# A gated attention and convolution block: channel sums accumulated in DRAM, and queue bounds in the output projection

## The chip, the cores and the metric

The kernel runs as one launch on one core of a Trainium2 chip. The core has a matrix engine (TensorE, PE in the profile, with its weight load PEld beside it), VectorE (DVE), ScalarE (ACT), GpSimd (POOL), and SyncE (SP), from which most transfers are issued. Transfers between DRAM and the on-chip memory SBUF run on 16 DMA engines, whichever engine issued them; PSUM is the small memory that PE writes its sums to. The metric is the device time of one execution in microseconds (us), lower is better.

## The reference

One decoder layer over 1024 tokens of width 1024, in float32. What matters here:

```
h = RMSNorm(x);  q, k, v, u, g = split(h @ w_in)
a = differential attention(q, k, v), 8 heads, RMS norm per head
y_a = a @ w_proj_attn
c = causal depthwise conv, width 31 (u_a * sigmoid(u_b)) + conv_b
c = silu(LayerNorm over the 1024 channels (c))
y_b = c @ w_proj_conv
x = x + (sigmoid(g_a) * y_a + sigmoid(g_b) * y_b) @ w_out
x = x + (silu(gate) * up) @ w_down,   gate, up = split(RMSNorm(x) @ w_gate_up)
```

The LayerNorm needs, for each token, the mean over all 1024 channels of the convolution's result. The channels lie in eight tiles of 128 partitions by 1024 tokens, so the mean begins with a sum over the eight tiles.

## The kernel before

**Products.** Each matrix product is made of three passes of PE over operands split in a high and a low part (hi*hi, hi*lo, lo*hi): `split_hi` (L120, on ACT) rounds a tile to its high part, `split_lo` (L125, on DVE) subtracts it from the tile for the low part. Weights arrive by DMA in a raw tile (`wraw`), are split into `whi` and `wlo` (three buffers each) and used; a `Stream` holds the splits two items ahead of their use (`ws.next()`). The output projection and the feed-forward use a seven-product scheme in place of eight block products, so that they also need sums and differences of blocks (`wless`, L1742, on DVE).

**Order.** The program's order is not the order in the queues: a planner that keeps simulated times puts the instructions of each engine in order, by what is ready in its simulation and by the place in the program. `after(ins)` adds one bound: what is traced under it is queued behind `ins`, if it is on the same engine. `last_mm`, `last_lo` and `last_of(engine)` name the latest PE product, low split or instruction of an engine. A queue, once made, runs strictly in its order.

**Convolution.** `conv_taps` (L565 to L589) handles one tile of 128 channels: `first_tap` (L575, ACT) writes the accumulator `acc`, 30 `tap`s (L581, DVE) add to it, and after the last one the result is stored to the DRAM tile `c_d[c]` (L587, SP). Tiles 0 to 3 have `acc` in PSUM and are copied first to an SBUF tile `done` (L585, ACT); tiles 4 to 7 have `acc` in SBUF. `done` and these `acc` share one tag with one buffer, so a tile's first tap waits until the tile before has left it. The taps are background work, handed out between the steps of the input projection and of attention, each lot behind the latest DVE instruction. In attention POOL does little but two small memsets per pair of query blocks (L1299 and L1300: one 128x128 block of each of `ph` and `pl`, the turned probabilities, is zeroed), which wait until the product `weigh` of the pair before has read these tiles.

**LayerNorm.** `ln_chunks(sb)` (from L1521) does one half of the tokens: it loads the eight tiles' halves `cc` from `c_d` (L1533), sums them into `s1` on DVE (L1535, seven additions), splits the sum and lets PE turn it into the mean, spread over the partitions (L1541). Then per tile: difference to the mean (L1547, DVE), square (L1548, ACT), its sum (L1551, DVE), and with the root scale, bias, sigmoid and product (L1566 to L1569) and the split to `cT_hi` and `cT_lo`. These steps are laid between the products of the attention projection, which has its own gates: `gated` (L1606, L1607) loads a gate and takes its sigmoid on ACT, `ya_out` (L1614) multiplies on DVE and so frees the PSUM tile. The first gates are bound behind `mean_hi`, the latest ACT instruction after the first step, which is the high split of the first half's `s1`. The convolution's projection follows on PE and reads `cT`, half after half.

**Output projection.** The loop over `WSEVEN` (from L1757) makes seven products z = 0 to 6 of 4 x 4 x 3 matmuls (L1804) into PSUM banks "a", "b" and "c"; "a" and "c" share four tiles, and after each product DVE adds the sums to the residual rows `xa` (L1814), which come by DMA (L1748). `wless` calls make weight differences at z = 1 and z = 3. From z = 5 on, `norm2` (L1699 to L1711) normalizes finished rows for the feed-forward: scale on DVE (L1703), transposes on PE (L1706), `split_hi` on ACT, `split_lo` on DVE, copy back on ACT (L1711). In z = 6 the `ws.next()` calls already split the first weights of the feed-forward (its gate product is L168 to L170 after the loop).

Of the kernel before, what the change touches and what calls it, by code (L numbers as in the profile page):

```python
# [10 lines left out]
F32 = mybir.dt.float32  # L11
F32R = mybir.dt.float32r
AF = mybir.ActivationFunctionType
ALU = mybir.AluOpType
AX = mybir.AxisListType

P = 128
S = 1024
# [39 lines left out]
def kernel(  # L58
# [321 lines left out]
    a_d = [dr.tile([P, S], F32, name=f"a_d{h}") for h in range(H)]  # L380
    u_d = [dr.tile([P, S], F32, name=f"u_d{c}") for c in range(NKT)]
    c_d = [dr.tile([P, S], F32, name=f"c_d{c}") for c in range(NKT)]
    g_d = [dr.tile([P, S], F32, name=f"g_d{c}") for c in range(2 * NKT)]
    ya_d = [dr.tile([P, S], F32, name=f"ya_d{c}") for c in range(NKT)]
    x2_d = [dr.tile([P, D], F32, name=f"x2_d{i}") for i in range(NT)]
# [181 lines left out]
    def conv_taps(c):  # L567
        acc = []

        def first_tap():  # L570
            if c < CONV_PSUM:
                acc.append(pcv[0].tile([P, S], F32, tag="acc", name=f"acc{c}", bufs=1))
            else:
                acc.append(cv.tile([P, S], F32, tag="acc", name=f"acc{c}", bufs=1))
            act.activation(acc[0][:], us[c][:], AF.Identity, bias=pcol("conv_b", c), scale=cw[:, c, CW - 1 : CW])  # L575

        def tap(t):
            def go():
                n = CW - 1 - t
                a_ = acc[0][:, n:]  # L580
                dve.scalar_tensor_tensor(a_, us[c][:, : S - n], cw[:, c, t : t + 1], a_, op0=ALU.mult, op1=ALU.add)  # L581
                if t == 0:
                    if c < CONV_PSUM:
                        done = cv.tile([P, S], F32, tag="acc", name=f"done{c}", bufs=1)
                        act.copy(done[:], acc[0][:])  # L585
                        acc[0] = done
                    nc.sync.dma_start(c_d[c][:], acc[0][:])  # L587

            return go  # L589

        return [first_tap] + [tap(t) for t in range(CW - 2, -1, -1)]
# [930 lines left out]
    def ln_chunks(sb):  # L1522

        cs = slice(sb * 512, (sb + 1) * 512)
        cc = [f32(cT_lo[:, c, cs]) for c in range(NKT)]

        def half(tag):
            return lp.tile([P, 512], F32, tag=tag, name=nm("ln" + tag), bufs=2)

        s1 = half("s")  # L1530
        for c in range(NKT):
            with after(last_at):
                nc.sync.dma_start(cc[c], c_d[c][:, cs])  # L1533
            if c:
                dve.tensor_tensor(s1[:], cc[0] if c == 1 else s1[:], cc[c], op=ALU.add)  # L1535
        mean = pm("mean") if sb else pln.tile([P, 512], F32, tag="mean", name=nm("mean"), bufs=1)
        s1h, s1l = [lp.tile([P, 512], F32R, tag="sq", name=nm(t_), bufs=2) for t_ in ("lnmh", "lnml")]
        split_hi(s1h[:], s1[:])
        split_lo(s1l[:], s1[:], s1h[:])
        for s_ in (s1h, s1l):  # L1540
            pe.matmul(mean[:], part[:], s_[:], start=s_ is s1h, stop=s_ is s1l)  # L1541
        yield
        s2 = half("s")
        for c in range(NKT):
            q = half("sq") if c else s2
            d = half("csg" if sb == 0 and c % 2 else "d")
            dve.tensor_tensor(d[:], cc[c], mean[:], op=ALU.subtract)  # L1547
            act.activation(q[:], d[:], AF.Square)  # L1548
            nc.sync.dma_start(cc[c], d[:])
            if c:  # L1550
                dve.tensor_tensor(s2[:], s2[:], q[:], op=ALU.add)  # L1551
            if c == 3:
                yield
        yield
        var = pm()
        for e in range(4):
            pe.matmul(var[:, e : e + 1], s2[:, e * P : (e + 1) * P], f32(part[:, 0:1]), start=True, stop=True)
        r = rsq8(var[:, :4], 1.0, 4)
        rb_ = pln.tile([P, 512], F32, tag="rstd", name=nm("rstd"), bufs=1)
        rw = half("sq")  # L1560
        dve.tensor_copy(rw[:].rearrange("p (e q) -> p e q", q=P), r.unsqueeze(2).to_broadcast([P, 4, P]))
        for e in range(4):
            pe.transpose(rb_[:, e * P : (e + 1) * P], rw[:, e * P : (e + 1) * P], ident[:])
        for c in range(NKT):
            z, sg = half("z"), half("csg")
            dve.tensor_tensor(z[:], cc[c], rb_[:], op=ALU.mult)  # L1566
            act.activation(z[:], z[:], AF.Identity, bias=pcol("ln_b", c), scale=pcol("ln_w", c))
            act.activation(sg[:], z[:], AF.Sigmoid)
            dve.tensor_tensor(z[:], z[:], sg[:], op=ALU.mult)  # L1569
            split_hi(cT_hi[:, c, cs], z[:])  # L1570
            split_lo(cT_lo[:, c, cs], z[:], cT_hi[:, c, cs])
            if c % 2:
                yield
# [120 lines left out]
    def rows_of(l):  # L1694
        s_ = ssq[l][0]
        dve.tensor_tensor(s_[:], s_[:], ssq[l][1][:], op=ALU.add)
        return rsq8(s_[:], 1.0 / D, 4)

    def norm2(t_, r, tp_):  # L1699

        for g in range(2):
            h = xa[t_][:, TOK[g]]
            dve.scalar_tensor_tensor(h, h, r[:, t_ % 4 : t_ % 4 + 1], wb2[:, TOK[g]], op0=ALU.mult, op1=ALU.mult)  # L1703
            pt = tp_()
            for k in range(4):
                pe.transpose(pt[:, k * P : (k + 1) * P], h[:, k * P : (k + 1) * P], ident[:])  # L1706
            src4 = pt[:].rearrange("p (k s) -> p k s", s=P)
            h_ = h2_hi[:, 4 * g : 4 * g + 4, t_ * P : (t_ + 1) * P]
            split_hi(h_, src4)
            split_lo(h2_lo[:, 4 * g : 4 * g + 4, t_ * P : (t_ + 1) * P], src4, h_)  # L1710
            act.copy(h, pt[:])  # L1711
# [48 lines left out]
    for z, (z_, b_, s_, (l, c), full) in enumerate(WSEVEN):  # L1760
        if z == 0:
            with after(last_of(mybir.EngineType.SP)):
                wload("12", (1, 0))
                wload("S3", (0, 1))
                wload("S1", (0, 0))
                wload("S4", (1, 1))
                x_rows(0)
                sload("S2")
                sload("S4")
                x_rows(1)  # L1770
                sload("S3")
        if z == 1:
            wless("S1", "S3", "S1")
        if z == 3:
            for q in range(2):
                room["22", q] = wraw()[:]
            wless("22", "12", "S2")
            for q in range(2):
                early_weights("22", q, 2 * q)
            wless("S3", "S4", "S3")  # L1780
        if z == 4:
            for j in (2, 3):
                early_weights("S3", j, 2 * j)
        start = s_ not in o
        if start:
            o[s_] = [p_.tile([P, 512], F32, tag=tag, name=nm("wo")) for p_, tag in wo_banks[s_]]
        for j in range(4):
            if z_ in ("S2", "S4", "S3") or j % 2 == 0:
                hi, lo = ws.next()
            if z == 1 and j == 2:  # L1790
                wless("S2", "S4", "S1")
            if z == 5 and j == 2:
                h2_hi = big.tile([P, NKT, S], F32R, tag="xhi", name="h2_hi")
                h2_lo = big.tile([P, NKT, S], F32R, tag="xlo", name="h2_lo")
            for i in range(4):
                t_ = slice(i * P, (i + 1) * P)
                if z_ in ("S2", "S4", "S3"):
                    A, B = [m_[:, t_] for m_ in (hi, lo)], [m_[:, 512:] for m_ in (hi, lo)]
                else:
                    r_, k_ = {"11": (0, 0), "12": (0, 1), "22": (1, 1), "S1": (1, 0)}[z_]  # L1800
                    A = [m_[2 * j + k_][:, TOK[r_]][:, t_] for m_ in (mT_hi, mT_lo)]
                    B = [m_[:, 512 * (j % 2) : 512 * (j % 2 + 1)] for m_ in (hi, lo)]
                for y_, (u_, v_) in enumerate(((0, 0), (0, 1), (1, 0))):
                    last_mm[0] = pe.matmul(  # L1804
                        o[s_][i][:], A[u_], B[v_], start=start and j + y_ == 0, stop=j == 3 and y_ == 2,
                        skip_group_check=not start,
                    ).ins
            for t_ in NORMS.get((z, j), ()):
                with after(last_mm[0]), after(last_add if z == 6 else None):
                    norm2(t_, r2[0], tr_first)  # L1810
        for i in range(4):
            t_ = 4 * l + i
            h = xa[t_][:, TOK[c]]
            last_add = dve.tensor_tensor(h, o[s_][i][:], h, op=ALU.add).ins  # L1814
            if full:
                nc.sync.dma_start(x2_d[t_][:, TOK[c]], h)
                squares(t_, c)
        if z in (4, 6):
            r2[l] = rows_of(l)
# [267 lines left out]
```

## Time and profile before

| | |
|---|---|
| three runs, median (lowest, highest) | 1738.96 us (1737.48, 1740.53) |
| the profiled execution, whole | 1737.98 us |
| its span, first to last instruction | 1736.2 us |
| mean granted TensorE clock | 0.999 |
| busy PE, PEld, DVE, ACT, POOL | 1718.1, 1479.1, 1283.6, 864.9, 211.7 us |

All times inside the execution are counted from the span's start. A group row names line, engine, operation, tiles and count, then busy time and mean duration in ns; a row of the timeline names start and duration in us, engine, line, operation, tiles and count, and in brackets the idle time of the engine before it and what ended that. In a row of a table by stage each engine's busy us stand in the order PE, PEld, DVE, ACT, POOL, each with its count in brackets, then the granted TensorE clock (1.00 is full), the DMA engines' busy share and GB/s.

In order of time: input projection with the first convolution tiles to about 310 us, attention with the others to about 822, attention projection with LayerNorm to 913, convolution's projection to about 1018, output projection to 1092, feed-forward to the end.

### The profile page before, as it was taken

The page shows a single profiled execution, that of the slowest core. Times are in us where ns is not written, and L with a number is a line of the kernel's source. Part 1 is how long each engine was busy: PE and PEld are TensorE (multiplying, and loading weights), DVE is VectorE, ACT ScalarE, POOL GpSimd, SP SyncE. Part 2 cuts the span into 40 slices and gives each one's busy share as a digit, 9 for nine tenths or more (in the row PEclk, how much of TensorE's full clock was granted, in tenths as well). Part 3 has the DMA queues.
Part 4 walks back from the last instruction along what each step waited for, and adds up shares of the span by engine and source line. Part 5 has one row for each costly group of instructions (what it writes and reads, how often), then busy time and mean ns, then how long its engine had stood idle before and what let it go on. Part 6 is the DMA issues. An engine that isn't in the chain of part 4 may idle for free.

```text
span 1736.2 us, 25867 instructions
## 1 busy us (share of the span) xinstructions
PE 1718.1 (99%) x9245; PEld 1479.1 (85%) x9245; DVE 1283.6 (74%) x2142; ACT 864.9 (50%) x1958; POOL 211.7 (12%) x200
## 2 busy tenths in 40 slices
PE   9999999999999999999999999999999999999999
PEld 7997889998998998988787878888888888888887
DVE  7575889898988988977788678866676666565554
ACT  5333335767776776856356325633333333333332
POOL 4997851000000000000000000000000000000000
PEclk9999999999999999999999999999999999999999
DMA  6343454334344344354873583135445444597663
GB/s 203 118 128 120 161 178 139 90 104 139 105 110 144 88 110 140 92 146 140 302 236 122 177 304 127 49 108 177 152 159 173 154 152 151 179 363 276 219 216 130
DMA packets 256325, 276.92 MB, mean 159 GB/s; under 512 B 16258, under 2 KB 178114, under 8 KB 256196
## 3 DMA queue, kind: packets, MB, share of 16 engines
q1 hardware_dynamic: 253920, 268.50, 48.2%
q0 software_dynamic: 1984, 5.72, 1.1%
q8 instruction: 73, 1.20, 0.3%
q10 hardware_dynamic: 292, 1.05, 0.1%
q14 instruction: 56, 0.46, 0.1%
HBM read 177.65 MB, written 81.30 MB: 149 GB/s over the span
## 4 chain that ended last, share of the span: by engine, by line
PE 89%; DVE 4%; DMA 3%; ACT 3%; issue 1%; SPq 0%; ACTq 0%; DVEq 0%
PE acc L962 30%; PE acc L481 12%; PE pg L170 11%; PE pg L168 11%; PE pg L169 11%; PE wo L1804 3%; PE sc L1271 2%; PE sc L1270 2%; PE pT L1309 2%; DVE acc L581 1%; PE pW L169 1%; PE pW L168 1%; PE pW L170 1%; PE pg L1088 1%; DMA room<-soS 1%
## 5 line engine op out<-in xcount | busy, mean ns | idle before, releaser
L581 DVE SCALAR_TENSOR_TENSOR acc<-u,cw,acc 128x1023 f32<-128x1023 f32 (+14 forms) x240 | 303.5, 1265 | 15.3 <-ACT acc L575 12.8
L168 PE MATMUL pg<-whi,hT_hi 128*128 128x256 f32 x704 | 199.9, 285 | 0.5 <-DVE v L125 0.5
L170 PE MATMUL pg<-whi,hT_lo 128*128 128x256 f32 x704 | 199.8, 284 | 0.0
L169 PE MATMUL pg<-wlo,hT_hi 128*128 128x256 f32 x704 | 199.4, 284 | 0.0
L125 DVE TENSOR_TENSOR wlo<-draw,whi 128x1024 fp32r<-128x1024 f32 x75 | 91.8, 1224 | 85.2 <-ACT whi L120 79.1
L120 ACT CAST whi<-draw 128x1024 fp32r<-128x1024 f32 x75 | 79.1, 1055 | 129.5 <-PE acc L481 119.3
L168 PEld LDWEIGHTS pg<-whi,hT_hi 128*128 128x128 f32 x704 | 133.9, 191 | 2.2 <-DVE v L125 0.7
L169 PEld LDWEIGHTS pg<-wlo,hT_hi 128*128 128x128 f32 x704 | 134.2, 191 | 1.8
L170 PEld LDWEIGHTS pg<-whi,hT_lo 128*128 128x128 f32 x704 | 134.2, 191 | 1.7
L120 ACT CAST whi<-wraw 128x1024 fp32r<-128x1024 f32 x90 | 94.5, 1052 | 73.0 <-PE pg L169 35.9
L481 PE MATMUL acc<-wlo,whi 128*128 128x512 f32 x308 | 119.8, 389 | 0.0
L481 PE MATMUL acc<-whi,wlo 128*128 128x512 f32 x308 | 119.8, 389 | 0.0
L168 PE MATMUL pg<-hT_hi,whi 128*128 128x512 f32 x288 | 114.6, 398 | 0.1
L169 PE MATMUL pg<-hT_lo,whi 128*128 128x512 f32 x288 | 114.1, 396 | 0.0
L170 PE MATMUL pg<-hT_hi,wlo 128*128 128x512 f32 x288 | 113.7, 395 | 0.0
L1277 ACT ACTIVATE E<-E,mn 128x640 f32<-128x640 f32 (+7 forms) x128 | 99.7, 779 | 27.6 <-DVE mn L1272 27.0
L120 ACT CAST whi<-s 128x1024 fp32r<-128x1024 f32 x54 | 56.8, 1052 | 107.2 <-PE acc L962 103.3
L125 DVE TENSOR_TENSOR wlo<-wraw,whi 128x1024 fp32r<-128x1024 f32 x75 | 92.5, 1236 | 12.7 <-ACT whi L120 12.0
L1272 DVE CUSTOM_DVE_ANT_0 E<-sc,tb 128x512 f32<-128x512 f32 (+3 forms) x128 | 74.2, 585 | 27.5 <-PE pT L1309 13.1
L962 PE MATMUL acc<-h_hi,whi 128*128 128x512 f32 x240 | 93.4, 389 | 0.0
L962 PE MATMUL acc<-h_lo,whi 128*128 128x512 f32 x240 | 93.4, 389 | 0.0
L962 PE MATMUL acc<-h_hi,wlo 128*128 128x512 f32 x240 | 90.1, 389 | 0.0
(371 smaller groups left out, 4587.8 us busy)
## 6 DMA issues: line engine op xcount, KB each, us to landing
wraw<-in_w_gate_up_dram SPq DMA_DIRECT2D x44, 512.0 KB, 4.8
wraw<-in_w_in_dram SPq DMA_DIRECT2D x40, 512.0 KB, 4.6
qs<-qs SPq DMA_DIRECT2D x96, 128.0 KB, 2.3
wd<-in_w_down_dram SPq DMA_DIRECT2D x44, 256.0 KB, 3.2
tdT<-wd SPq DMA_DIRECT2D x88, 128.0 KB, 4.7
draw<-sdS SPq DMA_DIRECT2D x44, 256.0 KB, 3.9
draw<-tdT SPq DMA_DIRECT2D x44, 256.0 KB, 3.7
wraw<-in_w_in_dram SPq DMA_DIRECT2D x32, 256.0 KB, 3.3
```

The lines of the kernel that those rows point to most:

```text
L120: act.copy(dst, src)
L125: last_lo[0] = dve.tensor_tensor(dst, src, f32(hi), op=ALU.subtract).ins
L168: pe.matmul(o, lh, rh, start=start, stop=False)
L169: pe.matmul(o, lh, rl, start=False, stop=False)
L170: last_mm[0] = pe.matmul(o, ll, rh, start=False, stop=stop).ins
L481: m = pe.matmul(o[s_][i][:], l_[:, ts], r_[:, 512:], start=start and j + y_ == 0, stop=j == n - 1 and y_ == 2, skip_group_check=not start,)
L581: dve.scalar_tensor_tensor(a_, us[c][:, : S - n], cw[:, c, t : t + 1], a_, op0=ALU.mult, op1=ALU.add)
L962: last_mm[0] = pe.matmul(o[:], a_[x_][:, k, :], b_[y_][:, k, :], start=start and k + x_ + y_ == 0, stop=k == 3 and x_ == 1, skip_group_che ...
L1270: pe.matmul(o[:, :w], qh[:, qs], k, start=True, stop=False)
L1272: dve.tensor_tensor_reduce(e[:, ks], o[:, :w], tb[:, S - nk + c0 : S - nk + c0 + w], 1.0, mn[:, j : j + 1] if c0 else 3.0e38, ALU.add, ALU ...
L1277: act.activation(e[:, :nk], e[:, :nk], AF.Exp, bias=mn[:, j : j + 1], scale=-1.0, accum_out=l[:, j : j + 1])
L1804: last_mm[0] = pe.matmul(o[s_][i][:], A[u_], B[v_], start=start and j + y_ == 0, stop=j == 3 and y_ == 2, skip_group_check=not start,).ins
```

## The change

- A new DRAM tile `cs_d` holds the sum over the eight convolution tiles. When a tile has ended it is stored to `c_d[c]` as before, and besides that tile 0 is stored to `cs_d` (SP), and tiles 1 to 7 are added to it by an accumulating DMA issued from POOL.
- `ln_chunks` loads `s1` from `cs_d` with one DMA, ahead of the eight loads of `cc`; the seven additions on DVE are gone, in both halves.
- In the output projection the `wless` of "22" (z = 3) and of "S2" (z = 1) are queued behind the latest low split.
- In z = 6, the DVE part of the splits that `ws.next()` makes is queued behind the latest DVE instruction, each matmul behind the one before it, and from the first `norm2` on each matmul of the loop behind the latest transpose.

```diff
--- before.py
+++ after.py
@@ -380,6 +380,7 @@
     a_d = [dr.tile([P, S], F32, name=f"a_d{h}") for h in range(H)]
     u_d = [dr.tile([P, S], F32, name=f"u_d{c}") for c in range(NKT)]
     c_d = [dr.tile([P, S], F32, name=f"c_d{c}") for c in range(NKT)]
+    cs_d = dr.tile([P, S], F32, name="cs_d")
     g_d = [dr.tile([P, S], F32, name=f"g_d{c}") for c in range(2 * NKT)]
     ya_d = [dr.tile([P, S], F32, name=f"ya_d{c}") for c in range(NKT)]
     x2_d = [dr.tile([P, D], F32, name=f"x2_d{i}") for i in range(NT)]
@@ -585,6 +586,10 @@
                         act.copy(done[:], acc[0][:])
                         acc[0] = done
                     nc.sync.dma_start(c_d[c][:], acc[0][:])
+                    if c:
+                        pool.dma_start(cs_d[:], acc[0][:], accum_op=ALU.add)
+                    else:
+                        nc.sync.dma_start(cs_d[:], acc[0][:])
 
             return go
 
@@ -1528,11 +1533,10 @@
             return lp.tile([P, 512], F32, tag=tag, name=nm("ln" + tag), bufs=2)
 
         s1 = half("s")
-        for c in range(NKT):
-            with after(last_at):
+        with after(last_at):
+            nc.sync.dma_start(s1[:], cs_d[:, cs])
+            for c in range(NKT):
                 nc.sync.dma_start(cc[c], c_d[c][:, cs])
-            if c:
-                dve.tensor_tensor(s1[:], cc[0] if c == 1 else s1[:], cc[c], op=ALU.add)
         mean = pm("mean") if sb else pln.tile([P, 512], F32, tag="mean", name=nm("mean"), bufs=1)
         s1h, s1l = [lp.tile([P, 512], F32R, tag="sq", name=nm(t_), bufs=2) for t_ in ("lnmh", "lnml")]
         split_hi(s1h[:], s1[:])
@@ -1696,6 +1700,8 @@
         dve.tensor_tensor(s_[:], s_[:], ssq[l][1][:], op=ALU.add)
         return rsq8(s_[:], 1.0 / D, 4)
 
+    last_tr = [None]
+
     def norm2(t_, r, tp_):
 
         for g in range(2):
@@ -1703,7 +1709,7 @@
             dve.scalar_tensor_tensor(h, h, r[:, t_ % 4 : t_ % 4 + 1], wb2[:, TOK[g]], op0=ALU.mult, op1=ALU.mult)
             pt = tp_()
             for k in range(4):
-                pe.transpose(pt[:, k * P : (k + 1) * P], h[:, k * P : (k + 1) * P], ident[:])
+                last_tr[0] = pe.transpose(pt[:, k * P : (k + 1) * P], h[:, k * P : (k + 1) * P], ident[:]).ins
             src4 = pt[:].rearrange("p (k s) -> p k s", s=P)
             h_ = h2_hi[:, 4 * g : 4 * g + 4, t_ * P : (t_ + 1) * P]
             split_hi(h_, src4)
@@ -1774,7 +1780,8 @@
         if z == 3:
             for q in range(2):
                 room["22", q] = wraw()[:]
-            wless("22", "12", "S2")
+            with after(last_lo[0]):
+                wless("22", "12", "S2")
             for q in range(2):
                 early_weights("22", q, 2 * q)
             wless("S3", "S4", "S3")
@@ -1786,9 +1793,11 @@
             o[s_] = [p_.tile([P, 512], F32, tag=tag, name=nm("wo")) for p_, tag in wo_banks[s_]]
         for j in range(4):
             if z_ in ("S2", "S4", "S3") or j % 2 == 0:
-                hi, lo = ws.next()
+                with after(last_of(mybir.EngineType.DVE) if z == 6 else None):
+                    hi, lo = ws.next()
             if z == 1 and j == 2:
-                wless("S2", "S4", "S1")
+                with after(last_lo[0]):
+                    wless("S2", "S4", "S1")
             if z == 5 and j == 2:
                 h2_hi = big.tile([P, NKT, S], F32R, tag="xhi", name="h2_hi")
                 h2_lo = big.tile([P, NKT, S], F32R, tag="xlo", name="h2_lo")
@@ -1801,10 +1810,11 @@
                     A = [m_[2 * j + k_][:, TOK[r_]][:, t_] for m_ in (mT_hi, mT_lo)]
                     B = [m_[:, 512 * (j % 2) : 512 * (j % 2 + 1)] for m_ in (hi, lo)]
                 for y_, (u_, v_) in enumerate(((0, 0), (0, 1), (1, 0))):
-                    last_mm[0] = pe.matmul(
-                        o[s_][i][:], A[u_], B[v_], start=start and j + y_ == 0, stop=j == 3 and y_ == 2,
-                        skip_group_check=not start,
-                    ).ins
+                    with after(last_mm[0] if z == 6 else None), after(last_tr[0]):
+                        last_mm[0] = pe.matmul(
+                            o[s_][i][:], A[u_], B[v_], start=start and j + y_ == 0, stop=j == 3 and y_ == 2,
+                            skip_group_check=not start,
+                        ).ins
             for t_ in NORMS.get((z, j), ()):
                 with after(last_mm[0]), after(last_add if z == 6 else None):
                     norm2(t_, r2[0], tr_first)
```

## The prediction

> **What bounds the kernel now.** I read the page first, then PE's own waits, then the timeline around each of them.
>
> ```profile
> span 1736.2 us, 25867 instructions
> PE 1718.1 (99%) x9245; PEld 1479.1 (85%) x9245; DVE 1283.6 (74%) x2142; ACT 864.9 (50%) x1958; POOL 211.7 (12%) x200
> ```
>
> PE is busy in all but 18.1 us (1736.2 less 1718.1), and the change removes no matmul. So nothing that DVE saves counts by itself: the prize is the part of PE's gaps that the edits reach. They lie in three places. The first is LayerNorm with the two projections beside it (a row of PE's waits, with sum, times and longest, then three rows of PE's timeline):
>
> ```profile
> PE pg L168 <- DVE gt L1614: 1.1, 1, 1.1
> 942.24 0.73 PE L168 MATMUL pg<-cT_hi,whi 128*128 128x512 f32 x2 [1.31 <-ACT cT_hi L120]
> ...
> 947.02 0.50 PE L168 MATMUL pg<-cT_hi,whi 128*128 128x512 f32 x1 [1.40 <-ACT whi L120]
> ...
> 949.42 0.50 PE L170 MATMUL pg<-cT_hi,wlo 128*128 128x512 f32 x1 [1.18 <-DVE wlo L125]
> ```
>
> That is 1.1 us while `ya_out` has yet to free a PSUM tile, and 1.31 + 1.40 + 1.18 = 3.9 us before the last convolution products. The second place is the output projection, by the table of stages:
>
> ```profile
> 944.00:948.00 4.00, 2.60 (x12) 1.66 (x10) 2.79 (x4) 3.02 (x5) 0.59 (x1) 1.00 0.38 131
> 1029.00:1033.00 4.00, 1.97 (x9) 1.10 (x7) 4.00 (x7) 1.04 (x1) 0.00 (x0) 1.00 1.04 406
> 1033.00:1037.00 4.00, 4.00 (x10) 2.71 (x11) 4.00 (x7) 1.30 (x4) 0.00 (x0) 0.57 1.04 416
> ```
>
> PE is idle for 2.0 of the 4 us from 1029 (4.00 less 1.97), and in the next 4 us its clock is 0.57, which costs 0.43 x 4 = 1.7 us more. The third is the hand-over to the feed-forward:
>
> ```profile
> 1093.40 0.85 PE L168 MATMUL pg<-h_hi,whi 128*128 128x512 f32 x2 [0.61 <-ACT h_hi L120]
> 1094.94 0.50 PE L169 MATMUL pg<-h_lo,whi 128*128 128x512 f32 x1 [0.69 <-DVE h_lo L125]
> ```
>
> That is 1.3 us. Together 1.1 + 3.9 + 3.7 + 1.3 = 10.0 us can be won at most, 0.6%.
>
> **LayerNorm's sum.** Removed are fourteen additions on DVE; added are two loads of 256 KB, each ahead of eight others on SP's queue.
>
> ```profile
> L1535 DVE TENSOR_TENSOR lns<-lns,cT_lo x12: 680/692/693, 839.8 to 858.5; 128x512 f32<-128x512 f32 x12
> L1535 DVE TENSOR_TENSOR lns<-cT_lo x2: 678/680/683, 839.1 to 851.6; 128x512 f32<-128x512 f32 x2
> 844.19 0.62 ACT L120 CAST lnmh<-lns 128x512 fp32r<-128x512 f32 x1 [6.19 <-DVE lns L1535]
> ...
> 859.33 0.62 ACT L120 CAST lnmh<-lns 128x512 fp32r<-128x512 f32 x1 [8.59 <-DVE lns L1535]
> 828.90 4.94 SPq L1533 DMA_DIRECT2D cT_lo<-c_d  x8
> DMA to landing us min/median/max: 5.0/5.5/5.8
> ```
>
> DVE loses 12 x 0.692 + 2 x 0.680 = 9.7 us of work, and ACT two waits, 6.19 + 8.59 = 14.8 us, behind which gates and squares are queued. The load of `s1` takes the place of the first `c_d` load, issued at 828.90, and lands by about 834.7 (+5.8). ACT has other work until 838.0 (844.19 - 6.19), so the first split comes 6 us earlier, the gates bound behind it are in time for `ya_out`, and **the 1.1 goes**. On SP the new load costs one issue (4.94 / 8 = 0.62) and on the DMA engines, at the 406 GB/s that the row of 1029 shows at full share, 256 KB take 0.65 us; by so much the `c_d` loads behind it come later. They are needed with the mean, which was made after 844.8 (844.19 + 0.62) before; loads issued by 834.5 are there by 840.3, so this is covered. Without that cover it would cost 0.65 us per half.
>
> For the 3.9 us the last `cT` must come sooner. PE interleaves the three products of the second half because it waits for `cT`; so they end together and give back their weight buffers late, and the waits for `whi` and `wlo` are the same lateness. The second `lnmh`, at 859.33 now, needs only a load that lands by about 845: some 14 us of the chain's start. I expect it to end about 10 us earlier. 1.3 us end the first wait; how many end the interleaving no row says. I take **all 3.9**, near the end that the size of the start argues for; bounds 1.3 and 3.9. Late next is nothing before the output projection, whose loads follow PE's own progress.
>
> **The convolution's sum.** Added are a store of 512 KB on SP, seven accumulating transfers of 512 KB, and their seven issues on POOL. No row shows an accumulating transfer. Nearest are the stores of `c_d`, the loads of `u`, and POOL's own transfers:
>
> ```profile
> u<-u_d SPq DMA_DIRECT2D x8, 512.0 KB, 4.3
> ...
> c_d<-done SPq DMA_DIRECT2D x4, 512.0 KB, 4.9
> c_d<-acc SPq DMA_DIRECT2D x4, 512.0 KB, 3.0
> ...
> t_d<-b_d POOLq DMA_DIRECT2D x8, 576.0 KB, 5.4
> L758 POOL DMA_DIRECT2D t_d<-b_d x8: 540/562/581, 153.8 to 274.6; - x8
> ```
>
> (The last number of the first four is the us from issue to landing.) The transfer reads the one buffer that the next first tap, on ACT, waits for:
>
> ```profile
> 312.73 1.25 ACT L575 ACTIVATE acc<-u,pvec,cw 128x1024 f32<-128x1024 f32 x1 [3.69 <-DMA c_d<-done]
> 547.41 1.24 ACT L575 ACTIVATE acc<-u,pvec,cw 128x1024 f32<-128x1024 f32 x1 [1.18 <-DMA c_d<-acc]
> 316.93 0.50 PE L1270 MATMUL sc<-ks,qs 128*128 128x512 f32 x1 [0.36 <-DVE mn L1272]
> 525.00:550.00 25.00, 25.00 (x141) 21.39 (x140) 20.77 (x54) 17.70 (x57) 0.36 (x2) 1.00 0.51 157
> 683.30 0.20 POOL L1300 MEMSET pl<- 128x128 f32 x1 [24.57 <-PE pW L169]
> L587 SPq DMA_DIRECT2D c_d<-acc x4: 320/386/535, 399.5 to 808.0; - x4
> ```
>
> Behind a waiting first tap stand ACT's exponentials and copies, behind the tap DVE's taps and minima, and PE waits for both. At 312 ACT's 3.69 us already cost PE 0.36, so each further us costs about one; at 547 the 1.18 cost PE nothing (25.00 of 25.00). Four hand-overs have this wait (tile 3 to 4, up to 6 to 7). Lower end: 0.4 us gained, if the planner puts other work ahead of the tap. Upper end: a load, a store and an issue one after the other, 4.3 + 4.9 + 0.6 = 9.8, 4.9 later than the store of `done`, at four places without cover: 19.6 lost. I take the nearest row, POOL's own transfer: 5.4 and 0.6 for the issue against 4.9, 1.1 later, and round it up for the sum to **1.5 lost**, at 312 alone. On POOL the transfer itself waits for the tile's end. Queued behind it are the memsets of L1300, for which `weigh` waits; they themselves wait some 24 us now, so POOL has the time. The last tile ends at 808.0 (L587), so even at the upper end `cs_d` is whole by 817.8, ahead of the first load at 828.9.
>
> The Trainium skill bears on that price: "Collectives: The Full Stack", section "The bandwidth ceiling: the fold count and why AG ≠ RS ≠ AR", has a sum inside the DMA engines cost nothing for the adding and much for its second source read. By it the transfer lies toward the upper end; no run shows that yet, and it stands beside the slower rival below.
>
> **The output projection's bounds.** Around 1030 DVE makes "22" weights, which are used last, between additions that free PSUM:
>
> ```profile
> 1028.64 1.28 DVE L1744 TENSOR_TENSOR wraw<-room 128x512 f32<-128x512 f32 x2
> 1029.85 1.22 DVE L125 TENSOR_TENSOR wlo<-room,whi 128x1024 fp32r<-128x1024 f32 x1
> 1030.98 0.68 DVE L1814 TENSOR_TENSOR xa<-wo,xa 128x512 f32<-128x512 f32 x1
> 1030.50 1.04 ACT L120 CAST whi<-room 128x1024 fp32r<-128x1024 f32 x1 [4.38 <-PE wo L1804]
> ```
>
> Two of them (1.28 us) stand right before the split and the first addition; with them gone the addition starts at about 1029.7. But the next weights' high part still ends at 1031.5 (1030.50 + 1.04), bound to PE's progress, so about 1.3 of the 2.0 idle stays: 0.7 won. A gap of that length at 947 left the clock at 1.00 (row of 944), so I count the 1.7 as won too: **2.4 won**. Bounds: 3.7 won, or 0.7 lost, since the "S2" differences are now behind a low split (1.22), and behind them waits the high split at 1030.50 that reads them.
>
> The Trainium skill, "TensorE: Matmul & The Clock Gate", section "Part 1: The HAM clock gate", lets the clock fall after an idle window of about 3.4 us; the rows show it fall after 2.0 idle in 4. By the page a shorter gap would cure nothing, and the term would be 0.7.
>
> **z = 6.** Splits of feed-forward weights leave DVE's way and transposes come before matmuls, so the last rows are ready sooner: 1.3 won. Against it, PE loses cover: it now runs matmuls of z = 6 while DVE scales the rows.
>
> ```profile
> 1078.20 0.39 PE L1804 MATMUL wo<-w22h,mTh 128*128 128x512 f32 x1
> 1075.61 1.23 DVE L125 TENSOR_TENSOR wlo<-wraw,whi 128x1024 fp32r<-128x1024 f32 x1 [1.18 <-ACT whi L120]
> 1077.62 2.73 DVE L1703 SCALAR_TENSOR_TENSOR xa<-xa,r,fnw_b 128x512 f32<-128x512 f32 x4
> ```
>
> Without the split at 1075.61 and its wait (2.4 us) the scaling ends at about 1078.0, just when z = 6 begins; but the transposes of the last two rows must find their PSUM tiles copied out, with all later matmuls now queued behind them. I take **0.5 won**; bounds 1.3 won and 2.7 lost (the whole scaling uncovered).
>
> The sum is 1.1 + 3.9 + 2.4 + 0.5 - 1.5 = 6.4 us less. The profiled execution took 1737.98 us, 1.8 over its span and 1.0 under the median of 1738.96; its gaps should stand for the median too. 1738.96 - 6.4 = 1732.6, **about 1732.5**, with a range of its own from 1729.5 to 1735.5.
>
> **Rivals.** (1) **No change**: the chain of LayerNorm moves, but a product or transfer that was close behind becomes the wait; then only 1.1 + 1.3 + 0.7 are won and 1.5 lost: 1737.4. For it: the DMA engines at their full share at 1029; against it: ACT's 14.8 us had no other cause. 0.25. (2) **Slower**: the accumulating transfer holds `acc`'s only buffer, by its two reads (as the page on collectives has it) or because it is issued late behind a waiting memset. Place: the four hand-overs. At 4.9 us later, with half a us of cover at three of them, it costs 4.9 + 3 x 4.4 = 18.1, and the time is 1738.96 - 7.9 + 18.1 = 1749; at 3 us later it costs 3 + 3 x 2.5 = 10.5, and the time is 1741.6. It decides from about 2.4 us later, where 2.4 + 3 x 1.9 = 8.1 eats the 7.9 of the other terms. For it: the place at 312 has no cover left; against it: three others have some, and the planner may put other work first. 0.17. (3) **All gaps go** and nothing is lost: 1738.96 - 10.0 = 1729.0. 0.13. The forecast has 0.45.
>
> A difference of under 0.2% (3.5 us) is about what a measurement of this kernel can't tell from no change. Faster (under 1735.5): the forecast and (3), 0.58. Same: (1) and a little of (2), 0.27. Slower (over 1742.4): most of (2), 0.15. The range runs from 1728 to 1743; below it lies some 0.05, above it, where (2) is strong, 0.12.
>
> **What would show it.** Right: no wait of ACT for L1535, the last `cT_hi` at least 8 us earlier, no waits at the three places of 942 to 949 and none of 1.1 for `gt`; clock 1.00 after the additions; accumulating transfers that land within 7 us, and waits at L575 of under 5 us. Wrong: PE gaps in attention of over 5 us in sum, or PE waiting for DVE or for transposes in z = 6.

## The result, and the profile after

The changed kernel takes **1750.4 us** (median of 6 runs, 1749.9 to 1751.4) beside 1739.7 us for the kernel before in the same comparison (1737.5 to 1740.9): 1.0064 of it, interval 1.0051 to 1.0077, so 10.6 us slower where 6.4 faster was forecast. The first two lines of its page, and then the largest of PE's own waits behind its start (engine, line and what it waited for; us in total, times, longest):

```profile
span 1749.0 us, 25887 instructions
PE 1719.7 (98%) x9245; PEld 1480.1 (85%) x9245; DVE 1273.7 (73%) x2128; ACT 860.9 (49%) x1958; POOL 217.5 (12%) x207
```

```profile
PE pg L168 <- ACT jk L787: 4.9, 4, 3.0
PE tr L1712 <- ACT xa L1717: 2.7, 1, 2.7
PE pg L168 <- DVE gt L1618: 2.5, 1, 2.5
PE wo L1814 <- ACT whi L120: 1.8, 1, 1.8
...
PE wo L1814 <- DVE xa L1824: 1.2, 1, 1.2
PE acc L967 <- POOL wlo L131: 1.0, 1, 1.0
```

DVE lost 9.9 us of work (1283.6 to 1273.7), about as forecast, and on balance it bought nothing: PE, with the same 9245 matmuls, waits for other things. (Lines behind the convolution's code are now 1 to 10 higher: L575 is L576, L1614 is L1618.) The division by stages tells where. A stage runs from its first matmul to the first of the next; us, with PE's idle time in brackets (differences are taken before rounding; the stages of before begin at 0, 308.5, 822.9, 915.8, 1008.5, 1093.4 and 1130.9):

| stage | before | changed | difference |
|---|---|---|---|
| start, to the first scores | 308.5 (4.0) | 310.4 (6.8) | +1.9 |
| attention | 514.5 (1.6) | 524.0 (8.3) | **+9.6** |
| attention's projection, LayerNorm beside it | 92.8 (1.1) | 99.2 (4.4) | **+6.3** |
| convolution's projection | 92.7 (4.0) | 87.0 (0.0) | **-5.7** |
| output projection | 84.9 (2.6) | 86.9 (5.9) | +2.0 |
| feed-forward, first products | 37.5 (0.7) | 36.4 (0.0) | -1.1 |
| the rest | 605.3 | 605.1 | -0.2 |

So the 3.9 us of waits at 942 to 949 are gone, and 17.8 us came ahead of them. (The two profiled spans lie 12.8 us apart, the medians 10.6: the profiled execution of before, 1737.98 us, was 1.8 under its median.) Idle time is not all: in the trace's clock records TensorE's clock, behind the first 13 us, is 1.00 but for stretches of 3.41 us at 0.50, each worth 1.7 us (3.41 x 0.5). The changed kernel has one in attention (419.7) and one in attention's projection (839.6); before has one, in the output projection (1033.1).

In attention, ACT's first taps (start, duration, what they waited for) are now:

```profile
316.48 1.24 ACT L576 ACTIVATE acc<-u,pvec,cw 128x1024 f32<-128x1024 f32 x1 [2.06 <-DMA cs_d<-done]
416.16 1.24 ACT L576 ACTIVATE acc<-u,pvec,cw 128x1024 f32<-128x1024 f32 x1 [2.86 <-DMA cs_d<-acc]
...
417.41 0.20 ACT L787 ACTIVATE jk<-pg 128x64 f32<-128x64 f32 x1
...
556.97 1.24 ACT L576 ACTIVATE acc<-u,pvec,cw 128x1024 f32<-128x1024 f32 x1 [2.25 <-DMA cs_d<-acc]
...
704.67 1.24 ACT L576 ACTIVATE acc<-u,pvec,cw 128x1024 f32<-128x1024 f32 x1 [1.80 <-DMA cs_d<-acc]
```

Each of the four waits for the accumulating transfer, 9.0 us in sum (2.06 + 2.86 + 2.25 + 1.80); before, two waited for stores, 4.9 us in sum (3.69 + 1.18). What such a wait costs PE is seen at 416: the copies `jk` of L787, which free PE's tiles `pg`, are queued on ACT behind the tap, and PE (its row, then the windows with PE's busy time and, third from the end, its granted clock) stands still and comes back at a lower clock:

```profile
420.10 0.80 PE L168 MATMUL pg<-hT_hi,whi 128*128 128x512 f32 x1 [2.98 <-ACT jk L787]
```

```profile
416.00:420.00 4.00, 1.12 (x6) 0.66 (x4) 2.21 (x9) 3.77 (x17) 0.00 (x0) 0.96 0.01 4
420.00:424.00 4.00, 3.90 (x11) 3.17 (x12) 4.00 (x9) 2.98 (x9) 0.00 (x0) 0.61 0.18 68
```

After attention, LayerNorm's first differences come ahead of the products `gt` that free PE's tiles:

```profile
861.71 0.69 DVE L1551 TENSOR_TENSOR lnd<-cT_lo,mean 128x512 f32<-128x512 f32 x1 [5.01 <-PE mean L1545]
...
863.51 0.68 DVE L1551 TENSOR_TENSOR lncsg<-cT_lo,mean 128x512 f32<-128x512 f32 x1
864.11 2.48 DVE L1618 TENSOR_TENSOR gt<-pg,gt 128x512 f32<-128x512 f32 x4
```

Four differences stand there. From 861.71 to 864.11 are 2.4 us, and PE's wait for `gt` is 2.5 where it was 1.1: the sum that is ready early has put its consumers in front (run 10 below shows it). Last, the windows of the places that the forecast had in the convolution's and output projection and in z = 6:

```profile
925.00:950.00 25.00, 25.00 (x114) 20.70 (x113) 18.12 (x29) 16.52 (x27) 0.00 (x0) 1.00 0.34 113
1041.00:1045.00 4.00, 2.82 (x13) 2.01 (x12) 4.00 (x8) 1.66 (x3) 0.00 (x0) 1.00 1.03 407
1045.00:1049.00 4.00, 4.00 (x19) 3.28 (x18) 2.99 (x5) 2.06 (x8) 0.00 (x0) 1.00 1.04 416
1060.00:1064.00 4.00, 2.20 (x10) 1.43 (x8) 4.00 (x5) 3.05 (x4) 0.00 (x0) 1.00 0.00 0
1094.00:1098.00 4.00, 1.31 (x11) 0.86 (x9) 2.78 (x5) 2.51 (x5) 0.00 (x0) 1.00 0.24 73
```

PE has no gap from 925 to 950. The first addition's gap, 2.0 before, is 1.2 (4.00 less 2.82) and the clock stays at 1.00; but a new one of 1.8 stands at 1060 (4.00 less 2.20), and one of 2.7 in z = 6.

### The profile page after: what moved, and what is told of

Same layout as the page of the kernel before. It is cut to its first block, busy times and chain, and to the rows that moved or that the text cites. A ratio compares the mean times of both kernels' runs of the same rounds, so it can differ in the third digit from the quotient of the medians.

```text
span 1749.0 us, 25887 instructions
## 1 busy us (share of the span) xinstructions
PE 1719.7 (98%) x9245; PEld 1480.1 (85%) x9245; DVE 1273.7 (73%) x2128; ACT 860.9 (49%) x1958; POOL 217.5 (12%) x207
## 5 line engine op out<-in xcount | busy, mean ns | idle before, releaser
L125 DVE TENSOR_TENSOR wlo<-wraw,whi 128x1024 fp32r<-128x1024 f32 x75 | 92.8, 1239 | 13.7 <-ACT whi L120 13.5
```

What stands on the lines that cost most here:

```text
L125: last_lo[0] = dve.tensor_tensor(dst, src, f32(hi), op=ALU.subtract).ins
```

## The experiments

The theory after the profile (**A**): the accumulating transfer reads `acc`'s one buffer and keeps it longer than the store does; the first taps, the copies behind them and PE follow. Against it stands **B**: the program sets its order anew with every edit, and another order alone might cost as much; and the bounds may carry part of the loss. A has two forms: the adding is what makes the transfer keep `acc` (A1), or a second reader of `acc` on POOL's queue does so without any adding (A2). By the names in the traces, every engine's queue is the same between the changed kernel and run 3, and between runs 7 and 9; the other pairs differ in order too. All times are medians; each ratio is to the kernel before on the same chip, with its 95% interval.

**1. The sums in DRAM alone** (the diff without its hunks from L1700 on).

> The sums in DRAM alone, without the bounds of the output projection and of z = 6. Theory A (the accumulating transfers hold the one buffer of acc, the first taps come late, and attention and what follows it lose): start, attention and attention's projection keep all that the changed kernel lost there (1.9, 9.6 and 6.3 us), and the convolution's projection keeps its 5.7 us won; without the bounds' 2.0 lost and 1.1 won the time is about 1749.5 us. Rival (the bounds matter as the prediction had them, 2.9 us won): 1753.3 us. Rival (the loss came with the bounds): 1734 us.

Measured: 1748.5 us, 1.0046 (1.0034 to 1.0058); start 311.5, attention 524.3, its projection 99.3, the convolution's 87.0. The loss, and the 5.7 us won, belong to the sums.

**2. The bounds alone** (only the diff's hunks from L1700 on).

> The bounds of the output projection and of z = 6 alone; LayerNorm's sum is made on DVE as before. Theory A has all the loss in the transfers: attention as before (PE idle about 1.6 us in it), output projection 2.0 us longer and feed-forward's first products 1.1 us shorter, together about 1740.6 us. The prediction's terms for the bounds (2.4 and 0.5 won) give 1736.8 us. If the bounds carried the loss, it is about 1750 us.

Measured: 1742.6 us, 1.0011 (1.0001 to 1.0021): not the 2.9 us won that the prediction had, but 0.11% lost, some 1.9 us. Attention is 513.8 with 1.4 of gaps. In z = 6 PE waits 2.9 us, until 1085.3, for the copies of transposed rows, and its clock falls (windows):

```profile
1084.00:1088.00 4.00, 2.67 (x11) 2.47 (x12) 1.49 (x3) 3.77 (x8) 0.00 (x0) 0.55 0.00 0
1088.00:1092.00 4.00, 4.00 (x14) 3.15 (x13) 0.69 (x1) 1.12 (x3) 0.00 (x0) 0.60 0.02 4
```

**3. Plain stores in place of the accumulating ones** (the kernel then leaves out the adding).

```
-                        pool.dma_start(cs_d[:], acc[0][:], accum_op=ALU.add)
+                        pool.dma_start(cs_d[:], acc[0][:])
```

> The seven accumulating transfers become plain stores on the same queue of POOL, with every instruction of each engine in the same order; left out is the adding of tiles 1 to 7 to the mean's sum. If the transfer's second read is what holds acc (theory A1), the stores land in 3 to 5 us, like before's stores of c_d, in place of 8.4; the 9.0 us of ACT's waits at the first taps go down to about 3, and attention loses about 3 us in place of 9.6: about 1742 us. If a second reader of acc on POOL's queue holds it as long without any adding (A2), or if it is the changed order of the instructions (theory B), the time stays at 1749 to 1751 us.

Measured: 1742.3 us, 1.0007 (0.9998 to 1.0016); by the two ratios 0.57%, 9.9 us, under the changed kernel. The issues and the time to landing of the accumulating transfers (changed kernel), then of the plain ones, and the plain kernel's first taps:

```profile
L590 POOL DMA_DIRECT2D cs_d<-acc x4: 863/864/873, 406.7 to 825.1; - x4
L590 POOL DMA_DIRECT2D cs_d<-done x3: 886/928/975, 204.0 to 308.4; - x3
...
DMA to landing us min/median/max: 7.4/9.0/10.0
```

```profile
L590 POOL DMA_DIRECT2D cs_d<-acc x4: 531/531/538, 405.0 to 816.0; - x4
L590 POOL DMA_DIRECT2D cs_d<-done x3: 572/574/578, 204.1 to 307.1; - x3
...
DMA to landing us min/median/max: 5.5/6.7/9.3
```

```profile
314.63 1.24 ACT L576 ACTIVATE acc<-u,pvec,cw 128x1024 f32<-128x1024 f32 x1 [1.44 <-DMA cs_d<-done]
411.68 1.24 ACT L576 ACTIVATE acc<-u,pvec,cw 128x1024 f32<-128x1024 f32 x1
548.74 1.24 ACT L576 ACTIVATE acc<-u,pvec,cw 128x1024 f32<-128x1024 f32 x1
694.26 1.24 ACT L576 ACTIVATE acc<-u,pvec,cw 128x1024 f32<-128x1024 f32 x1
```

This is the sharpest pair of the study: same instructions in the same order, same buffer, same queue. Only the adding differs: 0.3 us more per issue on POOL and 2.3 us more to landing (9.0 less 6.7; the plain ones had been expected after 3 to 5), and the taps' waits are 9.0 us with it and 1.4 without. The pages' rows of POOL's queue (packets, MB, share of the 16 engines' time; changed kernel, then this run) tell where the landing's time goes:

```profile
q0 software_dynamic: 2992, 9.39, 2.3%
```

```profile
q0 software_dynamic: 2992, 9.39, 1.7%
```

Packets and bytes are the same, but a packet of 4096 bytes takes 328 ns with the adding and 159 without (medians of the seven transfers' 896 packets in each trace). Theory A holds in its form A1, and B falls as the main cause. A smaller part stays open to it: attention is 516.2 here, 1.7 over before, with two waits for `jk` of 1.4 and 0.3 (at 389 and 377) that the changed kernel has too and before has not.

**4. Without the seven transfers** (the `pool.dma_start` line taken out; the sum is then tile 0 alone).

> The changed kernel without its seven accumulating transfers; left out is the adding of tiles 1 to 7 to the mean's sum (the sum is tile 0 alone). The planner is free to order the work anew. Theory A: start, attention and attention's projection are as before, and of the rest the 5.7 us won, the 2.0 lost and the 1.1 won remain: about 1739.7 - 4.8 = 1735 us. Theory B (the plan is thrown off by any such edit, by the loads and stores that stay as much as by the transfers): 1745 to 1751 us, with PE idle over 5 us in attention.

Measured: 1738.8 us, 0.9989 (0.9981 to 0.9998). Start 309.2 and attention 513.4 are as before and the convolution's projection is 87.0; but attention's projection takes 95.0, with the wait of 2.5 for `gt` still in it. That wait does not come from the transfers. By the medians the time is 2.3 us under before, where 4.8 had been expected; the 2.2 us that attention's projection still loses are most of the difference.

**5. Accumulating from DRAM**, in the changed kernel with its bounds:

```
-                        pool.dma_start(cs_d[:], acc[0][:], accum_op=ALU.add)
+                        pool.dma_start(cs_d[:], c_d[c][:], accum_op=ALU.add, max_dma_last_dim=1024)
```

> The changed kernel, with the seven accumulating transfers reading the tile that was just stored in DRAM in place of the buffer acc (in rows of 1024, half as long); the whole sum is made as in the changed kernel. If the second read of acc is the cause (theory A1), acc is freed by the plain store alone, ACT's waits at the first taps come down from 9.0 us to about the 5 us of the run without the transfers, and attention is as there: about 1739 us (within 0.2% of before). If it is the accumulating itself (its 0.9 us issues on POOL, its load on the DMA engines, the plan that makes room for it), the time stays at 1746 to 1751 us.

Measured: 1743.8 us, 1.0016 (1.0006 to 1.0027). Attention is 514.2 with 1.1 of gaps, as theory A has it: the adding is all there, `acc` is not held, and attention's 9.6 us are gone. (A transfer now goes in 512 packets of 1024 bytes in place of 128 of 4096, so source and packets changed together.) But the start is 314.4, 5.9 longer than before, by a cost that no theory had, and the time is 5 us over the 1739 expected. Its row on PE:

```profile
229.82 0.50 PE L967 MATMUL acc<-hT_hi,wlo 128*128 128x512 f32 x1 [3.69 <-POOL wlo L131]
```

**6. The first splits' bounds alone** (before, with only the two `after(last_lo[0])`).

> Before, with only the two bounds that put the differences for S2 and 22 behind a low split; nothing of z = 6. My theory: at 1031 the gap of 2.0 us goes down to 1.2 and the clock stays at 1.00 (1.7 won), and a new gap of 1.8 us near 1051 takes most of it, as in the run of all bounds: 0.5 to 1 us faster than before, and the order in z = 6 carries all of the loss of the bounds. Rival (the first splits' bounds carry it): 1.5 to 2 us slower than before, like the run of all bounds.

Measured: 1739.1 us, 0.9993 (0.9984 to 1.0001): 1.8 us under the median of before, 1.2 by the ratio, and no change at all lies within the interval too. In its trace the output projection takes 84.6 in place of 84.9: the gap at the first addition is 1.2 and the clock stays, but a new wait of 1.8 follows at 1052. Against all bounds (1.0011) the order in z = 6 costs 0.18%, some 3 us; the two intervals just meet.

**7. The sums from DRAM, no bounds** (runs 1 and 5 together).

> The sums in DRAM alone, read from the stored tile, with none of the bounds of the output projection and of z = 6. By theory A1 the run without transfers (1738.8 us, 2.3 under before) less the cost of the bounds (1.5 to 1.9): about 1737 us, 4 us under before. If reading from DRAM costs as much elsewhere: 1741 us or more.

Measured: 1742.1 us, 1.0007 (0.9998 to 1.0017): a miss. Attention 515.2, but the start 315.1, with PE's wait of 3.8 at 229.6.

**8. The gates first** (run 7, with the bounds of run 6 and this):

```
+            with after(first_gates if sb == 0 and c == 0 else None):
                 act.activation(q[:], d[:], AF.Square)
```

> As the run before it in this call, with the two bounds of the first splits, and with one bound more: the first square of LayerNorm's first half behind the first gates on ACT. Theory: in the changed kernel ACT has the square between the first gate and the other three, waits 6 us for it behind the mean's matmul, and so PE waits 2.5 us for gt; with the gates first this gap goes, and the time is about 1734 us, 7 us under before. If the gates are late by their loads: the gap stays at over 1 us, and the time is about 1736.5 us.

Measured: 1742.4 us, 1.0007 (0.9998 to 1.0016): a miss, and my theory of the gates falls. The four gates now run at 847.6 to 849.5, ahead of everything, and PE's wait for `gt` is 2.49 all the same. What is left in front of the products is what the rows at 861.71 show: four differences on DVE.

**9. The transfers issued one tile later in the program** (run 7 with this):

```
-                    if c:
-                        pool.dma_start(cs_d[:], c_d[c][:], accum_op=ALU.add, max_dma_last_dim=1024)
+                    for e in range(max(c - 1, 1), c if c < NKT - 1 else NKT):
+                        pool.dma_start(cs_d[:], c_d[e][:], accum_op=ALU.add, max_dma_last_dim=1024)
```

> As the sums read from DRAM without bounds (1742.1 us), but each accumulating transfer is issued one tile later, when its tile has long been stored (the last two at the last tile's end). Theory: there POOL waited 13.9 us for two stores of done in its queue, and behind it stood the low splits of weights, for which PE waited 3.8 us at 230; with the late issue POOL does not wait, the start goes back from 315.1 to about 309.5 us, attention stays at 514 to 515, and the time is about 1737 us, 4 us under before. Rival (the start is longer by the transfers' own load on the DMA engines or by POOL's 1.0 us issues): the start stays over 313 us and the time at 1741 to 1743.

Measured: 1743.0 us, 1.0012 (1.0003 to 1.002), start 315.0: a miss, and it tested nothing: no engine's queue differs from run 7, and POOL issued the first transfer at 206.0, where it was issued at 205.7. The order on POOL's queue follows what is ready, not the text. The rows ahead of PE's wait then pointed to a cause. Windows of before, of the changed kernel, of run 3 (plain stores) and of run 10 below, with the DMA engines' share and GB/s as the last two columns:

```profile
205.00:210.00 5.00, 5.00 (x23) 4.13 (x22) 4.91 (x5) 0.00 (x0) 2.06 (x1) 1.00 1.03 365
210.00:215.00 5.00, 5.00 (x23) 4.13 (x22) 4.26 (x5) 2.29 (x3) 2.64 (x3) 1.00 0.31 103
```

```profile
205.00:210.00 5.00, 5.00 (x24) 4.15 (x23) 4.89 (x6) 0.00 (x0) 4.25 (x4) 1.00 0.87 254
210.00:215.00 5.00, 5.00 (x23) 4.15 (x23) 3.82 (x4) 1.60 (x2) 0.00 (x0) 1.00 1.03 284
```

```profile
210.00:215.00 5.00, 5.00 (x24) 4.14 (x23) 3.82 (x4) 1.60 (x2) 0.00 (x0) 1.00 0.92 322
```

```profile
210.00:215.00 5.00, 5.00 (x24) 4.13 (x23) 3.82 (x5) 1.60 (x2) 0.00 (x0) 1.00 1.06 244
```

POOL's wait for the weights, before and in the changed kernel:

```profile
212.28 1.29 POOL L943 TENSOR_TENSOR s<-wraw 128x512 f32<-128x512 f32 x1 [5.22 <-DMA wraw<-in_w_in_dram]
```

```profile
217.64 1.29 POOL L948 TENSOR_TENSOR s<-wraw 128x512 f32<-128x512 f32 x1 [8.39 <-DMA wraw<-in_w_in_dram]
```

At 205 two loads of weights, two stores of `t_d` and a store of `u_d` share the DMA engines. Before, the engines are at 0.31 from 210 on. With tile 1's accumulating transfer among them the engines stay full to 215 and move 244 to 284 GB/s where they moved 365 at the same share, the weights come 5 us later to POOL (217.64 against 212.28), and PE waits at 230 for POOL's split: 1.0 us in the changed kernel, 3.5 to 4.6 in the runs from DRAM. Not all of the lateness is the adding: with the plain stores of run 3 the engines move 322 GB/s at 0.92, the weights reach POOL at 215.97, and PE does not wait. Why the same lateness costs so unequally is not settled.

**10. The differences behind the first products** (run 9, with the bounds of run 6 and this, `prods` being the products of `ya_out`):

```
+            with after(prods[1] if sb == 0 and c == 0 else None):
                 dve.tensor_tensor(d[:], cc[c], mean[:], op=ALU.subtract)
```

> As the run before it in this call, with the two bounds of the first splits (1.8 us under before by themselves) and LayerNorm's first differences on DVE behind the first two products of ya_out. Theory: since the sum is there early, DVE has four differences (2.4 us) ahead of the products that free PSUM, and PE waits 2.5 us for them; behind the products they cost PE at most the 1.1 us of before. Then the attention projection is 1.4 us shorter than in the run before it, and the time is about 1734 us, 7 us under before. Rival (the differences then come late for the convolution's projection): its wait of 3.9 us comes back, and the time is about 1737 us.

Measured: 1739.0 us, 0.9985 (0.9977 to 0.9994), the first version with the whole sum that is under the kernel before by more than its interval, by 2.0 us where 7 had been expected. Attention's projection is 92.4 in place of 96.7, with 0.3 of gaps and no wait for `gt`; the convolution's stays at 87.1. The start is still 314.9, 6.4 longer than before.

**11. The transfers bound on POOL** (run 10 with this):

```
                     for e in range(max(c - 1, 1), c if c < NKT - 1 else NKT):
+                        with after(last_of(mybir.EngineType.Pool)):
                             pool.dma_start(cs_d[:], c_d[e][:], accum_op=ALU.add, max_dma_last_dim=1024)
```

> As the run with the late differences (1739.0 us, 2.0 under before), but each accumulating transfer is bound on POOL's queue behind the work that stood there at the end of the next tile, so that tile 1's no longer runs at 205 to 215 us, where the DMA engines were full and the loads of weights landed 3 us later. Theory: the loads then land as before, POOL's splits are in time, PE's wait of 3.5 us at 229 and the clock it cost go, the start ends at about 309.5 in place of 314.9 us, and the time is about 1734 us, 7 us under before. Rival (the load moves to another full place, or the wait at 229 has another cause): the start stays over 312 us and the time at 1737 or more.

Measured: **1734.4 us, 0.9965 (0.995 to 0.9979)**, 5.8 us under the kernel before and, by the two ratios, 0.99% or some 17 us under the changed one. Its transfers, its window at 210 and its products:

```profile
L591 POOL DMA_DIRECT2D cs_d<-c_d x7: 1003/1012/1106, 236.8 to 812.3; - x7
```

```profile
210.00:215.00 5.00, 5.00 (x24) 4.14 (x23) 3.82 (x4) 1.68 (x3) 1.07 (x1) 1.00 0.54 189
```

```profile
845.62 0.69 DVE L1622 TENSOR_TENSOR gt<-pg,gt 128x512 f32<-128x512 f32 x1 [2.37 <-PE pg L170]
848.11 0.69 DVE L1622 TENSOR_TENSOR gt<-pg,gt 128x512 f32<-128x512 f32 x1 [1.80 <-PE pg L170]
848.72 0.68 DVE L1553 TENSOR_TENSOR lnd<-cT_lo,mean 128x512 f32<-128x512 f32 x1
```

The first transfer goes out at 236.8, the engines are at 0.54 at 210 to 215, and PE's wait at 229 is gone but for 0.2; the start is 310.4, 4.5 shorter than in run 10. In the start hardly anything else moved (1801 of PE's 1802 instructions and 134 of POOL's 138 stand in the order of run 10), so these 4.5 belong to the transfers' place. The start is 0.9 longer than the 309.5 expected; a wait of 1.2 at 281 for `qkraw` stands in it, 0.3 before.

A second buffer for `acc`, which would free the tap without another read of DRAM, was not tried.

## Why the prediction was wrong, step by step

- **The convolution's sum: the step that failed.** It had "1.5 lost, at 312 alone". The price came from POOL's own transfers (5.4 us to landing); the accumulating ones land after 9.0. And the place was wrong: at 312 the wait even shrank, 3.69 to 2.06, while the three hand-overs that I had given cover wait 2.86, 2.25 and 1.80. Attention lost 9.6 us; 7.9 of them go when the adding goes (run 3), and all of them when the transfer reads the stored copy (run 5). The rival "slower" had this mechanism and, with 4.9 us later, 18.1 us and 1749; the first three stages lost 17.8 and the time is 1750.4. That the numbers agree so well is chance: only attention's part came by that mechanism. Of the start's 1.9, a wait of 1.0 at 230 comes with the full DMA engines, for which I had no term at all; another of 0.9 at 302, which before has not, is there in run 3 too. In attention's projection the wait for `gt` is 1.4 longer, by the differences on DVE (run 10), and two waits of 0.76 for attention's result, at 836.8 and 838.1, and one of 0.4 stand ahead of 1.7 us lost at half clock; the other 1.3 of that stage's 6.3 are not accounted for. Those two waits may come of a convolution that ends 17 us later than before (last sum issued at 825.1, where the last store stood at 808.0); no run took them alone.
- **The Trainium skill's rule** in "Collectives: The Full Stack", section "The bandwidth ceiling: the fold count and why AG ≠ RS ≠ AR", that a sum in the DMA engines pays for its second source read, stood beside the rival. The runs agree with it in size: 328 ns a packet against 159 for the plain store, 9.0 us to landing against 6.7. That the second read is the reason, and not another part of the adding, no run shows.
- **LayerNorm's chain: the waits went, but not by the step forecast.** The forecast had the chain end about 10 us earlier. The last splits `cT_hi` of before and of the changed kernel:

```profile
L120 ACT CAST cT_hi<-lnz x16: 602/620/624, 898.2 to 942.4; 128x512 fp32r<-128x512 f32 x16
```

```profile
L120 ACT CAST cT_hi<-lnz x16: 601/618/627, 902.8 to 954.8; 128x512 fp32r<-128x512 f32 x16
```

Counted from the first product of attention's projection (822.9, 834.5, and 823.9 in run 11), the second `lnmh` comes after 36.4 us before, 32.0 in the changed kernel and 26.3 in run 11; the last `cT_hi` after 119.5, 120.4 and 116.5. So 10 us at the chain's start became 3 at its end in run 11, and none in the changed kernel. There the convolution's projection itself begins later against the chain, so that the last `cT_hi` starts 21.2 us behind its first product where it was 26.6: the 5.7 won in it stand against 6.3 lost just ahead, and the two projections take 186.2 us together, 185.5 before. In run 11 they take 180.5, and the gain is real.
- **The wait for `gt`: 1.1 won, measured 1.4 lost.** I had asked what is late next only of gates and loads; the early mean also releases its own consumers, and on one DVE these came first.
- **The output projection's bounds: 2.4 won was right for the place and wrong for the stage.** At the first addition the gap went from 2.0 to 1.2 and the clock stayed, about 0.8 + 1.7 = 2.5. But a wait of 1.8 came up 20 us later, and in run 11 the clock fell behind that one (0.75 and 0.82 from 1045 to 1053). Both together can't be told from nothing (run 6: 0.3 us won in the stage, and an interval with 1 in it).
- **z = 6: 0.5 won, measured about 3 lost.** The lower bound of 2.7 was the right mechanism, copies of transposes with all matmuls queued behind them; I chose the other end because the scaling seemed done in time, and the copies on ACT were not. In the changed kernel the wait is 2.7 us, and 1.3 of the old waits went; in run 2 a wait of 2.9 and 6.83 us at half clock (0.55 and 0.60 in the windows) took it past the bound.

With the transfers' hold, their place at 205, the order of the differences and z = 6 mended, run 11 is 5.8 us under before, near the 6.4 forecast, but not by the forecast's sum: by the profiles the two projections win 5.1 us and attention 1.0, while the output projection, where 2.4 were to be won, takes 2.2 longer and the start 1.9.

## What to carry to other kernels

A sum made by accumulating DMAs takes work off an engine but keeps its source buffer longer than a plain store from the same queue does, here by 2.3 us; look at who waits for that buffer, and where there is one only, let the transfer read the stored copy. Then look at where it is issued: it keeps the DMA engines busy for some 3 us more (their share from 210 to 215 went from 0.31 to 1.03), and a load that something waits for must not be among its neighbours. And when a chain is made to end earlier, its consumers come earlier too, and may stand in front of the work that frees the bottleneck's tiles.

## What the hardware showed beside it

- An accumulating transfer of 512 KB from SBUF was issued by POOL in 0.86 to 0.98 us, a plain one in 0.53 to 0.58, and one that reads DRAM in 1.0 to 1.1. Its packets of 4096 bytes took 328 ns each, twice the 159 of the plain one.
- The granted clock did not follow the length of a gap. In the changed kernel 2.7 us idle in the window from 1094 were followed by 1.00, and 1.8 at 1060 too; in run 2, 2.9 us idle gave 0.55 and 0.60. The window behind the first of these:

```profile
1098.00:1102.00 4.00, 4.00 (x24) 3.42 (x23) 1.39 (x2) 3.10 (x7) 0.00 (x0) 1.00 0.02 4
```

Nor did it follow the program. PE's wait of 2.5 us for `gt` is in eight of the profiles, and in five of them the clock fell there. Runs 7 and 9 have the same queues: from 857 to 861 the clock is 1.00 in run 7 and 0.74 in run 9. In the traces of these runs a fall is 0.50 for 3.41 us, or for 6.83, so it costs 1.7 or 3.4 us; that much of a difference between two profiles can be the clock alone.

The Trainium skill, "TensorE: Matmul & The Clock Gate", section "Part 1: The HAM clock gate", has an idle window of about 3.4 us ahead of a fall. The traces differ: falls came here behind 2.0 us idle in 4 (before, at 1029), and in the changed kernel at 839.6 behind waits of 0.76, 0.76 and 0.4, while 2.7 us passed without one. What tells the cases apart, these runs don't show. A term for the clock in a forecast is thus worth a range, not a value.
